# Where the sums of W_down's blocks are made: four sets in attention, eight in mix, two in W_o, none in W_up

## The chip, the cores and the metric

The kernel runs on one core of a Trainium2 chip. The metric is the device time of one execution in microseconds (us), lower is better. Engines are named as in the profile: PE multiplies matrices, DVE is the vector engine, ACT the scalar engine, POOL GpSimd, and SP issues nearly all DMAs of this kernel.

## The reference: one layer of a hybrid decoder

With 512 tokens, a model width of 1024 and a feed-forward width of 4096, all in float32:

```python
h = rms_norm(x, g_pre_mix)
q, k, v, cb, cc, cu, ga, gc = split(h @ w_in)          # 512 x6, 1024 x2
y_attn = stick_breaking_attention(q, k, v) @ w_attn_out  # 8 heads of 64, causal
y_conv = (cb * causal_depthwise_conv(cc * cu, w_conv)) @ w_conv_out
m = sigmoid(ga + b) * y_attn + sigmoid(gc + b) * y_conv
x = x + rms_norm(m @ w_o, g_post_mix)
f = square(relu(rms_norm(x, g_pre_mlp) @ w_up)) @ w_down
x = x + rms_norm(f, g_post_mlp)
x = x + sigmoid(rms_norm(x, g_ple) @ w_ple_gate) * (p @ w_ple_proj)
```

## The kernel before: stages, queues and sums

Every matrix product is split into a high and a low float32r part, three matmuls for one (lines 91 to 93). A weight block of 512 KB is loaded by SP into one of 4 buffers `raw` (line 71); ACT makes the high part `whi` by a cast (line 64), and DVE subtracts to get the low part `wlo` (line 65). The same two lines split everything else: `wth`/`wtl` (the transposed attention weights), `oyh`/`oyl` (the attention output), `st`, `us`. The split weights and the tiles of the sums below share one pool of 15 buffers.

The stages follow each other on PE: the head (norm, v), attention in four steps j of two heads each, mix in eight steps j (gates, convolution and attention output projections), W_o, W_up, W_down, and a last part. W_up and W_down use a Strassen-like scheme with seven products; W_down's right-hand side needs, beside blocks of W_down itself, four sums of blocks for each of 16 sets. `make_sums` (line 296) makes one set, long ahead of W_down: it lets SP issue the saves of the set before (line 292, two of 512 KB from `w` to `wsum` in DRAM), then two loads of 512 KB of `in_w_down_dram` into `w` (line 303), and then the engine that is passed makes four subtractions of 128x512 (line 309).

PE and SP run in program order. On DVE, ACT and POOL a scheduler sets the order when the kernel is built; each of them then runs its list in order, so an instruction that waits for its input holds all that stand behind it. `tc.high_priority(-LATE)` lowers the priority of what is made under it, so that the scheduler puts it behind other work that it thinks ready.

Before the change the 16 sets are made: two in the head and two in attention (steps 1 and 2), all at low priority on DVE; eight in mix, steps 0 and 1 at low priority on DVE, steps 2 to 7 on POOL; three in W_o, one on POOL before block k=0 and one on DVE before k=1 and before k=3; and one on DVE in W_up, in the middle of chunk 4 (the save follows in chunk 6).

What else the prediction speaks of, by its line before the change (from the middle of the attention loop on, lines stand two to ten lower after it). The loop of attention (line 430) makes step j's scores, the convolution, and then the transposes of the two heads' weights (`wtrans`, whose splits are `wth` and `wtl`), with a projection between them to keep PE busy: in the last step, j=3, these are the gates of mix, `gate(0,0)`, `gate(0,1)` and `gate(1,0)` (sigmoid at line 421). `av` (line 388) then multiplies head by head, and line 392 and 393 with a split make `oyh` and `oyl`. In mix, step j takes two gates, one block with the rows of `w_conv_out` and `w_attn_out` (two loads of 256 KB into one `raw`), twelve matmuls of the convolution part, twelve of the attention part and three multiplications and additions (lines 485, 489, 490). Step 0's convolution part is followed by `gate(1,1)`, and then by the attention part, whose last three matmuls use `oyh`, `oyl` of the last two heads. In W_up, `up_load` loads two blocks per chunk and combines them on DVE (669, 671, 672, 673) before they are split into `us`, and after the products DVE adds at lines 695, 701, 703 (and 711 every fourth chunk). Those adds release the PSUM buffers that PE writes next.

Of the kernel before, what the change touches and what calls it, by code (L numbers as in the profile page):

```python
# [25 lines left out]
LATE = 150  # L26
# [7 lines left out]
def hybrid_block(ctx, tc, x, p, g_pre_mix, w_in, b_gate, w_conv, w_attn_out, w_conv_out, w_o,  # L34
                 g_post_mix, g_pre_mlp, w_up, w_down, g_post_mlp, g_ple, w_ple_gate, w_ple_proj, out):
    nc = tc.nc
# [20 lines left out]
    def bank():  # L57
        return psp.tile([P, 512], F32, tag="ps", name="ps")

    def tm(dt=F32):  # L60
        return tmp.tile([P, 512], dt, tag="tmp", name="tmp")
# [18 lines left out]
    def w4(dt=F32):  # L80
        return wts.tile([P, 2, 512], dt, tag="w", name="w4")
# [207 lines left out]
    def save_sums():  # L289
        while unsaved:  # L290
            dst, src = unsaved.pop(0)
            nc.sync.dma_start(dst, src)
# [3 lines left out]
    def make_sums(eng=None):  # L296
        eng = eng or nc.gpsimd
        save_sums()
        j = next(made)
        q = []  # L300
        for h in range(2):
            t = w4()
            nc.sync.dma_start(t, wd[j][h].rearrange("p (c n) -> p c n", c=2))
            q += [t[:, 0], t[:, 1]]
        dst = wsum[j // 2][:, :, j % 2, :]
        o = [w4(), w4()]
        t1, t2, t3, t4 = (o[i // 2][:, i % 2] for i in range(4))
        for r, x_, y_ in ((t1, q[1], q[0]), (t2, q[3], t1), (t3, q[3], q[1]), (t4, q[2], t2)):
            eng.tensor_tensor(r, x_, y_, op=ALU.subtract)
        unsaved.extend([(dst[:, 0:2], o[0]), (dst[:, 2:4], o[1])])  # L310
# [7 lines left out]
    def proj_q(j):  # L318
        st = bigt([P, 4, S], name="st")
        split(st[:, 0], st[:, 1], proj(wcols(w_in, j * P), hx))  # L320
        return st

    def proj_k(j, st):
        split(st[:, 2], st[:, 3], proj(wcols(w_in, 512 + j * P), hx))
# [38 lines left out]
    def wtrans(w):  # L363
        wh = bigt([P, 1280], name="wth")
        wl = bigt([P, 1280], name="wtl")
        for group in ((0,), (1, 3), (2,)):
            ps = bank()
            base = WBLK[group[0]][0]
            n = 0
            for kb in group:  # L370
                c0 = WBLK[kb][0] - base
                for qb in range(kb, NT):
                    o = BLK[qb][0] + kb * P
                    nc.tensor.transpose(ps[:, c0 + (qb - kb) * P:c0 + (qb - kb + 1) * P], w[:, o:o + P], ident)
                n += WBLK[kb][1]
            split(wh[:, base:base + n], wl[:, base:base + n], ps[:, 0:n])
        return wh, wl
# [4 lines left out]
    def av(h, wt, of):  # L382
        ps = bank()
        for kb in range(NT):
            c0, n = WBLK[kb]
            lhs = v2[kb // 2][:, kb % 2, h, :]
            for i in range(2):
                nc.tensor.matmul(ps[:, kb * P:S], lhs, wt[i][:, c0:c0 + n], start=(kb == 0 and i == 0),
                                 stop=(kb == NT - 1 and i == 1))
        r, o = (slice(0, 64), slice(64, 128)) if h % 2 == 0 else (slice(64, 128), slice(0, 64))  # L390
        sh = tm()
        nc.scalar.copy(sh[r], ps[o])
        nc.vector.tensor_tensor(of[r], ps[r], sh[r], op=ALU.add)
        if h % 2 == 1:
            split(oy_h[0][:, h // 2], oy_l[0][:, h // 2], of)

    def conv_c(c):
        ps = proj(wcols(w_in, 2048 + c * P), hx)
        ct = tm()
        nc.scalar.copy(ct, ps)  # L400
        return ct

    def conv_u(c, ct):
        ps = proj(wcols(w_in, 2560 + c * P), hx)
        nc.vector.tensor_tensor(ct, ct, ps, op=ALU.mult)
        y = tm()
        wc = [cols[:, 16 + i * 4 + c:17 + i * 4 + c] for i in range(3)]
        nc.vector.tensor_scalar(y, ct, wc[2], None, op0=ALU.mult)
        for i, d in ((1, 1), (0, 2)):
            nc.vector.scalar_tensor_tensor(y[:, d:S], ct[:, 0:S - d], wc[i], y[:, d:S], op0=ALU.mult, op1=ALU.add)  # L410
        return y

    def conv_b(c, y):
        ps = proj(wcols(w_in, 1536 + c * P), hx)
        nc.vector.tensor_tensor(y, ps, y, op=ALU.mult)
        split(oy_h[1][:, c], oy_l[1][:, c], y)

    def gate(j, which):
        ps = proj(wcols(w_in, 3072 + 1024 * which + j * P), hx)
        sg = tm()  # L420
        nc.scalar.activation(sg, ps, AF.Sigmoid, bias=cols[:, 8 * which + j:8 * which + j + 1])
        return sg
# [9 lines left out]
    for j in range(4):  # L432
        wa, wb = scores(st)
        y = conv_u(j, ct)
        conv_b(j, y)
        if j < 3:
            st = proj_q(j + 1)
        else:
            sg[0] = gate(0, 0)
        ta = wtrans(wa)  # L440
        if j < 3:
            proj_k(j + 1, st)
        else:
            sg[1] = gate(0, 1)
        tb = wtrans(wb)
        if j < 3:
            ct = conv_c(j + 1)
        else:
            next_gate = gate(1, 0)
        of = tm()  # L450
        if j in (1, 2):
            with tc.high_priority(-LATE):
                make_sums(nc.vector)
        av(2 * j, ta, of)
        av(2 * j + 1, tb, of)

# [11 lines left out]
        return lambda k: (oy_h[part][:, k, :], oy_l[part][:, k, :])  # L468

    for j in range(NK):  # L470
        if j > 1:
            make_sums()
        else:
            with tc.high_priority(-LATE):
                make_sums(nc.vector)
        sa, sc = sg if j == 0 else (next_gate if j == 1 else gate(j, 0), last_gate if j == 1 else gate(j, 1))

        def two(t, j=j):
            return [(t[:, 4 * i:4 * i + 4], w[:, j * P:(j + 1) * P].rearrange("(k p) m -> p k m", p=P))
                    for i, w in ((1, w_conv_out), (0, w_attn_out))]  # L480

        wo2 = weights(two, [P, NK, P])
        save_sums()
        py = proj(wo2, oyc(1), 4, 4)
        nc.vector.tensor_tensor(sc, sc, py, op=ALU.mult)
        if j == 0:
            last_gate = gate(1, 1)
        py = proj(wo2, oyc(0), 4, 0)
        nc.vector.tensor_tensor(sa, sa, py, op=ALU.mult)
        nc.vector.tensor_tensor(sa, sa, sc, op=ALU.add)  # L490
        split(m_h[j // 4][:, j % 4], m_l[j // 4][:, j % 4], sa)
        if j == 3:
            for t in range(NT):
                nc.sync.dma_start(xr[t // 2][:, t % 2, :], x[t * P:(t + 1) * P, :])
        if j == 6:
            nc.sync.dma_start(pf, p[0].rearrange("(t p) d -> p t d", p=P))
            nc.sync.dma_start(wpr, w_pp.rearrange("(k p) m -> p k m", p=P))
            split(wph, wpl, wpr)
        if j == 7:
            for kk in range(2):  # L500
                ps = bank()
                for t in range(NT):
                    nc.tensor.transpose(ps[:, t * P:(t + 1) * P], pf[:, t, kk * P:(kk + 1) * P], ident)
                split(pt[:, kk], pt[:, 2 + kk], ps)


    def rows(nk, stat, w, tail, chain):
        acc = {}
        held = {}
        for k in range(nk):  # L510
            if k in (0, 1, 3):
                make_sums(nc.gpsimd if k == 0 else nc.vector)
            if k == 4:
                save_sums()
            wk = wrow(w, k)
            if k >= nk - tail:
                held[k] = wk
                continue
            sh, sl = stat(k)
            for t in range(NT):  # L520
                tok = slice(t * P, (t + 1) * P)
                for hf in range(2):
                    if k == 0:
                        acc[t, hf] = bank()
                    cs = slice(hf * 512, (hf + 1) * 512)
                    mm3(acc[t, hf], sh[:, tok], sl[:, tok], wk[0][:, cs], wk[1][:, cs], k == 0, False)
        for t in range(NT):
            tok = slice(t * P, (t + 1) * P)
            for hf in range(2):
                cs = slice(hf * 512, (hf + 1) * 512)  # L530
                for k in range(nk - tail, nk):
                    sh, sl = stat(k)
                    wk = held[k]
                    mm3(acc[t, hf], sh[:, tok], sl[:, tok], wk[0][:, cs], wk[1][:, cs], False, k == nk - 1)
            chain(t, [acc[t, 0], acc[t, 1]])
# [184 lines left out]
    for _, c, n in order:  # L720
        if n == 6 and c + 1 < NJ:
            up_load(c + 1)
            if c == 4:
                make_sums(nc.vector)
            if c == 6:
                save_sums()
        up_mm(c, n)


# [188 lines left out]
```

## Time and profile before

| what | us |
|---|---|
| median of 3 runs (lowest, highest) | 741.13 (738.96, 741.35) |
| the profiled execution, its own time | 740.71 |
| its span (first to last instruction) | 738.9 |
| PE busy | 727.5 (98%) |
| DVE busy | 515.3 (70%) |
| ACT busy | 378.0 (51%) |
| POOL busy | 98.0 (13%) |

A time in the profile is counted from the start of the span. The timeline gives the start and length of one instruction or of a run of like ones (x3), the engine, the line, what it writes and reads, and in square brackets for how long the engine sat idle before it and what ended that. SPq rows are DMA issues: their length is the time on SP's queue, not that of the transfer. A matmul is pipelined: its length (0.39 us) is longer than the distance to the next one (0.23 us), and the distance is what counts.

### The profile page before, as it was taken

To read this page: it belongs to the slowest core of one execution; us is meant where nothing else is said; L and a number is where in the kernel's file an instruction comes from. 1 tells how busy PE (TensorE), PEld (TensorE's weight loads), DVE (VectorE), ACT (ScalarE), POOL (GpSimd) and SP (SyncE) were. 2 spreads that over 40 slices of the span, in tenths; PEclk is the share of its full clock that TensorE was granted. 3 is DMA by queue.
4 is the path that set the end of the run, shared out by engine and by line. 5 is a ranking of instruction groups with operands and counts; after the bars stand their busy time and mean duration, and the time that the engine had idled before them with its cause. 6 is when DMAs were issued, how large, how long until landed. Compare 5 with 4: busy or idle time off the path is not lost. (4 is left out here: it accounts for less than half of the span.)

```text
span 738.9 us, 10316 instructions
## 1 busy us (share of the span) xinstructions
PE 727.5 (98%) x3976; PEld 630.1 (85%) x3976; DVE 515.3 (70%) x640; ACT 378.0 (51%) x595; POOL 98.0 (13%) x124
## 2 busy tenths in 40 slices
PE   8999999999899999999999999999999999999997
PEld 7888888888688888888899999999988888888886
DVE  6768696967445433844889898967699878268762
ACT  6364546351334221433855696757777467256431
POOL 1105052332442222001100000000000000001100
PEclk9999999999999999999999999999999999999999
DMA  8593717163997867861425544523455767577311
GB/s 313 178 252 112 204 53 228 34 199 120 295 323 254 279 204 256 309 204 65 155 95 169 174 115 115 149 81 93 165 170 177 231 232 225 183 239 273 122 57 58
DMA packets 112105, 132.29 MB, mean 179 GB/s; under 512 B 4116, under 2 KB 82744, under 8 KB 111032
## 3 DMA queue, kind: packets, MB, share of 16 engines
q1 hardware_dynamic: 111464, 127.43, 53.9%
q10 hardware_dynamic: 592, 4.20, 1.4%
q8 instruction: 31, 0.51, 0.3%
q14 instruction: 18, 0.15, 0.1%
HBM read 108.55 MB, written 23.07 MB: 178 GB/s over the span
## 5 line engine op out<-in xcount | busy, mean ns | idle before, releaser
L65 DVE TENSOR_TENSOR wlo<-raw,whi 128x512 fp32r<-128x512 f32 (+1 forms) x84 | 78.4, 955 | 66.5 <-ACT whi L64 41.1
L91 PE MATMUL ps<-h1h,whi 128*128 128x512 f32 x288 | 113.3, 393 | 0.0
L93 PE MATMUL ps<-h1h,wlo 128*128 128x512 f32 x288 | 112.2, 390 | 0.0
L92 PE MATMUL ps<-h1l,whi 128*128 128x512 f32 x288 | 112.2, 389 | 0.0
L64 ACT CAST whi<-raw 128x512 fp32r<-128x512 f32 (+1 forms) x84 | 64.6, 809 | 54.9 <-PE ps L93 20.6
L91 PE MATMUL ps<-w,sb 128*128 128x512 f32 x216 | 84.1, 389 | 0.0
L93 PE MATMUL ps<-w,sb 128*128 128x512 f32 x216 | 84.0, 389 | 0.0
L92 PE MATMUL ps<-w,sb 128*128 128x512 f32 x216 | 84.0, 389 | 0.0
L65 DVE TENSOR_TENSOR w<-raw,w 128x1024 fp32r<-128x1024 f32 x56 | 67.6, 1219 | 21.3 <-PE ps L92 10.2
L64 ACT CAST w<-raw 128x1024 fp32r<-128x1024 f32 x56 | 58.5, 1052 | 34.7 <-PE ps L93 14.1
L133 POOL TENSOR_TENSOR rs<-ms,mhalf 128x1 f32<-128x1 f32 x20 | 14.9, 744 | 419.9 <-DVE ms L129 366.4
L91 PE MATMUL ps<-h2h,us 128*128 128x256 f32 x224 | 63.6, 284 | 1.2 <-DVE tmp L701 1.2
L91 PEld LDWEIGHTS ps<-h1h,whi 128*128 128x128 f32 x288 | 54.1, 188 | 11.5
L93 PEld LDWEIGHTS ps<-h1h,wlo 128*128 128x128 f32 x288 | 54.1, 188 | 11.3
L92 PE MATMUL ps<-h2l,us 128*128 128x256 f32 x224 | 63.4, 283 | 0.0
L93 PE MATMUL ps<-h2h,us 128*128 128x256 f32 x224 | 63.4, 283 | 0.0
L92 PEld LDWEIGHTS ps<-h1l,whi 128*128 128x128 f32 x288 | 54.1, 188 | 10.8
L65 DVE TENSOR_TENSOR us<-raw,us 128x1024 fp32r<-128x1024 f32 x42 | 50.5, 1218 | 6.8 <-ACT us L64 6.7
L64 ACT CAST us<-raw 128x1024 fp32r<-128x1024 f32 x42 | 43.3, 1050 | 19.7 <-DVE raw L673 9.4
L93 PEld LDWEIGHTS ps<-w,sb 128*128 128x128 f32 x216 | 40.5, 188 | 8.5
L92 PEld LDWEIGHTS ps<-w,sb 128*128 128x128 f32 x216 | 40.5, 188 | 8.5
L91 PE MATMUL ps<-tb,us 128*128 128x256 f32 x168 | 47.7, 284 | 0.0
(206 smaller groups left out, 1654.2 us busy)
## 6 DMA issues: line engine op xcount, KB each, us to landing
raw<-in_w_in_dram SPq DMA_DIRECT2D x36, 512.0 KB, 6.4
w<-in_w_down_dram SPq DMA_DIRECT2D x32, 512.0 KB, 4.5
wsum<-w SPq DMA_DIRECT2D x32, 512.0 KB, 3.4
raw<-in_w_up_dram SPq DMA_DIRECT2D x32, 512.0 KB, 4.7
raw<-wsum SPq DMA_DIRECT2D x32, 512.0 KB, 5.2
raw<-in_w_down_dram SPq DMA_DIRECT2D x24, 512.0 KB, 4.1
raw<-in_w_o_dram SPq DMA_DIRECT2D x8, 512.0 KB, 5.8
raw<-in_w_ple_gate_dram SPq DMA_DIRECT2D x8, 512.0 KB, 6.3
```

Of the source, the lines that this page charges most:

```text
L64: a = nc.scalar.copy(hi, src)
L65: b = nc.vector.tensor_tensor(lo, src, hi.bitcast(F32), op=ALU.subtract)
L91: nc.tensor.matmul(ps, lh, rh, start=start, stop=False, skip_group_check=onto)
L92: nc.tensor.matmul(ps, lh, rl, start=False, stop=False, skip_group_check=onto)
L93: nc.tensor.matmul(ps, ll, rh, start=False, stop=stop, skip_group_check=onto)
L133: nc.gpsimd.tensor_tensor(r, m, mhalf, op=ALU.pow)
```

## The change

In attention a set is made in each of the four steps, at normal priority and not at low. In mix the sets stay in the same steps on the same engines, those of steps 0 and 1 at normal priority now. In W_o the set on POOL before block 0 is gone; in W_up the set of chunk 4 and its saves in chunk 6 are gone. There are 16 sets as before; DVE makes 40 subtractions (36 before), POOL 24 (28 before). PE's instructions keep their order.

```diff
@@ attention, end of each step j
         of = tm()
-        if j in (1, 2):
-            with tc.high_priority(-LATE):
-                make_sums(nc.vector)
+        make_sums(nc.vector)
         av(2 * j, ta, of)
         av(2 * j + 1, tb, of)
@@ mix
     for j in range(NK):
-        if j > 1:
-            make_sums()
-        else:
-            with tc.high_priority(-LATE):
-                make_sums(nc.vector)
+        make_sums(nc.gpsimd if j > 1 else nc.vector)
@@ rows(), which W_o uses
-            if k in (0, 1, 3):
-                make_sums(nc.gpsimd if k == 0 else nc.vector)
+            if k in (1, 3):
+                make_sums(nc.vector)
@@ W_up
         if n == 6 and c + 1 < NJ:
             up_load(c + 1)
-            if c == 4:
-                make_sums(nc.vector)
-            if c == 6:
-                save_sums()
         up_mm(c, n)
```

Three places show what the scheduler makes of it. The first is SP's list at the end of attention. Before the change it holds there, from the gate block of `gate(1,1)` on, the sets of mix 1 (`w_1920`, `w_1922`, saved as `w_1924`, `w_1925`) and mix 2 (`w_1972`, `w_1974`), and, at the line with x2, the blocks of `gate(2,0)` and `gate(2,1)`:

```order
L71 DMA raw<-in_w_in_dram 128x8x128
L303 DMA w_1920<-in_w_down_dram 128x1024
L303 DMA w_1922<-in_w_down_dram 128x1024
L71 DMA raw<-in_w_conv_out_dram 128x4x128
L71 DMA raw<-in_w_attn_out_dram 128x4x128
L292 DMA wsum_377<-w_1924 128x2x512
L292 DMA wsum_377<-w_1925 128x2x512
L303 DMA w_1972<-in_w_down_dram 128x1024
L303 DMA w_1974<-in_w_down_dram 128x1024
L71 DMA raw<-in_w_in_dram 128x8x128 x2
L71 DMA raw<-in_w_conv_out_dram 128x4x128
L71 DMA raw<-in_w_attn_out_dram 128x4x128
```

After the change, from the gate block of `gate(1,1)` on, which here too stands behind the saves of mix 0's set, with mix 1's set (`w_1944`, `w_1946`, saved as `w_1948`, `w_1949`) and mix 2's (`w_1996`, `w_1998`):

```order
L71 DMA raw<-in_w_in_dram 128x8x128
L303 DMA w_1944<-in_w_down_dram 128x1024
L303 DMA w_1946<-in_w_down_dram 128x1024
L71 DMA raw<-in_w_conv_out_dram 128x4x128
L71 DMA raw<-in_w_attn_out_dram 128x4x128
L292 DMA wsum_378<-w_1948 128x2x512
L292 DMA wsum_378<-w_1949 128x2x512
L303 DMA w_1996<-in_w_down_dram 128x1024
L303 DMA w_1998<-in_w_down_dram 128x1024
L71 DMA raw<-in_w_in_dram 128x8x128 x2
L71 DMA raw<-in_w_conv_out_dram 128x4x128
L71 DMA raw<-in_w_attn_out_dram 128x4x128
```

The rows read alike, since the list is the same from here on; but one set more (that of attention's step 3) stands ahead of it now, so that mix 0's set stands in time where mix 1's stood, and the block of `gate(1,1)` and all that follows come one set later. The blocks of `gate(2,0)` and `gate(2,1)` still follow the saves of mix 1's set and the loads of mix 2's.

The second place is ACT's list at the end of attention, from the sigmoid of `gate(0,0)` (the first row at line 421) on. There are two groups of `wth` (heads 6 and 7), and `whi` of 128x1024 are gate blocks. Before:

```order
L421 ACTIVATE tmp<-ps,cols 128x512
L64 CAST wth<-ps 128x512 x2
L64 CAST wth<-ps 128x256
L64 CAST whi<-raw 128x1024
L421 ACTIVATE tmp<-ps,cols 128x512
L64 CAST wth<-ps 128x512 x2
L64 CAST wth<-ps 128x256
L64 CAST whi<-raw 128x1024
```

After, from the row ahead of that sigmoid on:

```order
L64 CAST whi<-raw 128x1024
L421 ACTIVATE tmp<-ps,cols 128x512
L64 CAST wth<-ps 128x512 x2
L64 CAST wth<-ps 128x256
L64 CAST whi<-raw 128x512 x2
L421 ACTIVATE tmp<-ps,cols 128x512
L64 CAST wth<-ps 128x512 x2
L64 CAST wth<-ps 128x256
L421 ACTIVATE tmp<-ps,cols 128x512
L64 CAST whi<-raw 128x1024
L392 COPY tmp<-ps 64x512
L64 CAST whi<-raw 128x1024
```

The first `whi` of 128x1024 is now the block of `gate(1,1)`, ahead of the sigmoid. Between the two groups of `wth` stood the block of `gate(2,0)`; now the block of mix 1's `w_conv_out` and `w_attn_out` stands there, and the two blocks of `gate(2,0)` and `gate(2,1)` follow behind, on both sides of a copy of the last heads' output.

The third place is DVE's list in W_up around the set that is removed (`w_3764`, `w_3766`). Before:

```order
L65 TENSOR_TENSOR us<-raw,us 128x1024
L309 TENSOR_TENSOR w_3768<-w_3764 128x512
L711 TENSOR_TENSOR af<-af 128x4x256
L309 TENSOR_TENSOR w_3768<-w_3766,w_3768 128x512
L309 TENSOR_TENSOR w_3769<-w_3766,w_3764 128x512
L309 TENSOR_TENSOR w_3769<-w_3766,w_3768 128x512
L701 TENSOR_TENSOR tmp<-ps,tmp 128x256
L65 TENSOR_TENSOR us<-raw,us 128x1024
L695 TENSOR_TENSOR tmp<-ps,tmp 128x256
L669 TENSOR_TENSOR s_3879<-raw 128x512
```

After, two chunks further on (lines 663, 665 to 667, 689, 695 are before's 669, 671 to 673, 695, 701; the first column of sums of a chunk is `s`):

```order
L65 TENSOR_TENSOR us<-raw,us 128x1024 x2
L665 TENSOR_TENSOR raw<-s_4004,raw 128x512
L65 TENSOR_TENSOR us_4016<-s_4004,us_4016 128x512
L666 TENSOR_TENSOR raw<-raw 128x512
L667 TENSOR_TENSOR raw<-raw 128x512
L663 TENSOR_TENSOR s_4127<-raw 128x512
L65 TENSOR_TENSOR us<-raw,us 128x1024
L695 TENSOR_TENSOR tmp<-ps,tmp 128x256
L65 TENSOR_TENSOR us<-raw,us 128x1024
L689 TENSOR_TENSOR tmp<-ps,tmp 128x256
```

The four subtractions are gone, and the scheduler puts the first step of the next chunk's loads (`s`, which waits for a DMA) ahead of the adds at 695 and 689 of the chunk that PE is working on.

## The prediction

> **What bounds the kernel now.** I read the page's head first, then PE's waits, then the work in windows of 20 us, then the timeline where a window is short of work. The page says that PE is the bound:
>
> ```profile
> span 738.9 us, 10316 instructions
> PE 727.5 (98%) x3976; PEld 630.1 (85%) x3976; DVE 515.3 (70%) x640; ACT 378.0 (51%) x595; POOL 98.0 (13%) x124
> ```
>
> So a subtraction that is moved between DVE, POOL and stages costs or saves nothing in itself. Only PE's waits count. The list of PE's waits, longest first, names those that the change can reach:
>
> ```profile
> PE ps L388 <- ACT wth L64: 1.9, 1, 1.9
> ...
> PE ps L91 <- DVE tmp L701: 1.2, 2, 0.6
> PE ps L388 <- DVE wtl L65: 1.1, 1, 1.1
> ```
>
> Two places: the product of head 7 at the end of attention (line 388), called stall A here, and the add at line 701 in W_up, stall B. The windows (PE busy and matmuls, PEld, DVE, ACT, POOL, granted clock, DMA share, GB/s) show that A costs more than its idle time:
>
> ```profile
> 180.00:200.00 20.00, 16.99 (x77) 14.02 (x76) 10.19 (x15) 7.46 (x13) 6.84 (x6) 0.91 0.91 286
> ...
> 181.00:193.00 12.00, 8.99 (x45) 7.29 (x44) 4.17 (x7) 4.60 (x8) 5.03 (x4) 0.97 1.08 333
> ```
>
> 3.0 us are idle in the first window, at a mean clock of 0.91. PE's timeline through A:
>
> ```profile
> 187.26 0.39 PE L388 MATMUL ps<-wth,v 128*128 128x512 f32 x1
> ...
> 188.36 0.27 PE L388 MATMUL ps<-wtl,v 128*128 128x128 f32 x1
> 190.56 0.50 PE L388 MATMUL ps<-wth,v 128*128 128x512 f32 x1 [1.93 <-ACT wth L64]
> 192.15 0.69 PE L388 MATMUL ps<-wtl,v 128*128 128x512 f32 x1 [1.08 <-DVE wtl L65]
> ...
> 194.02 0.73 PE L91 MATMUL ps<-oyh,whi 128*128 128x512 f32 x1
> 194.55 0.63 PE L92 MATMUL ps<-oyl,whi 128*128 128x512 f32 x1
> ...
> 196.01 0.40 PE L93 MATMUL ps<-oyh,wlo 128*128 128x512 f32 x1
> 196.25 0.40 PE L91 MATMUL ps<-oyh,whi 128*128 128x512 f32 x1
> ```
>
> Head 6's eight matmuls run from 187.26 to the next start at about 188.43, 1.17 us. Head 7's would do the same and end at 189.60; five matmuls at the normal distance (0.23, 196.01 to 196.25) would bring the sixth of mix to 190.75. It starts at 196.01. Stall A costs 5.3 us: 3.0 idle, 2.3 of matmuls spaced 0.3 to 0.5 us until 195.8.
>
> Its cause is an order. ACT, DVE and SP at that place:
>
> ```profile
> 178.33 0.68 ACT L421 ACTIVATE tmp<-ps,cols 128x512 f32<-128x512 f32 x1
> 178.91 1.33 ACT L64 CAST wth<-ps 128x512 fp32r<-128x512 f32 x3
> 188.40 1.04 ACT L64 CAST whi<-raw 128x1024 fp32r<-128x1024 f32 x1 [8.15 <-DMA raw<-in_w_in_dram]
> ...
> 189.94 1.33 ACT L64 CAST wth<-ps 128x512 fp32r<-128x512 f32 x3
> ```
>
> ```profile
> 179.49 0.68 DVE L309 TENSOR_TENSOR w<-w,w 128x512 f32<-128x512 f32 x1
> 180.09 1.61 DVE L65 TENSOR_TENSOR wtl<-ps,wth 128x512 fp32r<-128x512 f32 x3
> 189.54 1.95 DVE L65 TENSOR_TENSOR wlo<-raw,whi 128x1024 fp32r<-128x1024 f32 x1 [7.83 <-ACT whi L64]
> 191.41 1.60 DVE L65 TENSOR_TENSOR wtl<-ps,wth 128x512 fp32r<-128x512 f32 x3
> ```
>
> ```profile
> 175.94 4.63 SPq L292 DMA_DIRECT2D wsum<-w  x2
> 180.62 1.34 SPq L303 DMA_DIRECT2D w<-in_w_down_dram  x2
> 182.05 1.07 SPq L71 DMA_DIRECT2D raw<-in_w_in_dram  x2
> ```
>
> ACT sits 8.15 us before the cast of the block of gate(2,0), with head 7's `wth` behind it in the list. That block was issued at 182.05 and landed at 188.40. SP stood ahead of it at the second save of mix 1's set until the last subtraction of that set had ended (179.49 + 0.68 = 180.17; the save went out by 180.57). So a set's last sum, late on DVE, holds SP, SP holds a gate's block, the block holds ACT, and ACT holds head 7.
>
> **The change part by part.** *Stall A.* The rows of the new order put head 7's `wth` behind the block of w_conv_out and w_attn_out of mix 1, not behind that of gate(2,0), and one set earlier on SP. My walk through the new lists, on before's clock: the two scans with their products,
>
> ```profile
> 162.34 2.88 DVE L354 TENSOR_TENSOR_SCAN keep<-keep,ends 128x1280 f32<-128x1280 f32 x1 [0.68 <-POOL keep L351]
> ...
> 171.31 1.49 DVE L355 TENSOR_TENSOR beta<-beta,keep 128x1279 f32<-128x1279 f32 x1 [0.61 <-POOL beta L351]
> ```
>
> take 10.5 us. A `wlo` of 1.2 us is no longer ahead of them, so they run from about 161.0 to 171.5; two short steps of the convolution and mix 0's last sum follow and end at 172.6 to 173.3. The save goes out, gate(1,1)'s block leaves at 173.7 and mix 1's loads behind it. What such transfers take:
>
> ```profile
> DMA to landing us min/median/max: 4.2/5.2/8.4
> ...
> DMA to landing us min/median/max: 2.7/3.7/5.3
> ```
>
> (the first row is that of the weight blocks between 150 and 200 us, the second that of the sums' loads and saves there). With 1.0 MB of saves, 0.5 of gate block, 1.0 of loads and 0.5 of the mix block at 333 GB/s, behind each other, gate(1,1) lands at 178.5, mix 1's two loads at 180.2 and 181.8, its block by 183.4. ACT then casts that block and does head 7's `wth` (1.33) by about 186.0; they are due at 188.4, where head 7 follows head 6. DVE makes the four sums of mix 1 between 182.5 and 184.9, two `wlo` of 0.6, and the first piece of `wtl` by 187.4, due at 188.66. The slack is 2.4 us on ACT and 1.3 on DVE. Stall A goes: **-5.3 us**.
>
> What would come of gate(1,1)'s block standing ahead of gate(0,0)'s sigmoid: that sigmoid frees a bank for gate(1,0). It ran at 178.33 before and would now end at 180.0. gate(1,0), 24 matmuls of 0.23 us ahead of head 6 at 187.26, starts at 181.7: no cost, with 1.7 us of slack.
>
> A rule against this size: the Trainium skill (TensorE: Matmul & The Clock Gate, What's actually happening) has the clock fall to half only after an idle window of about 3.4 us. By that rule two waits of 1.93 and 1.08 us with matmuls between would leave the clock alone, A would cost 3.0 and the forecast would be 2.3 us higher, 737.8. The rows disagree: 0.53 us from 194.02 to 194.55, with no wait there. The sum goes by the rows.
>
> *A new wait in mix 0.* The last three matmuls of its attention part read `oyh`, `oyl` of heads 6 and 7. On before's clock:
>
> ```profile
> 205.34 0.39 PE L92 MATMUL ps<-oyl,whi 128*128 128x512 f32 x1
> ```
>
> That is the matmul that reads that `oyl`; without A it stands at 205.34 - 5.3 = 200.0. Before, the split was done early:
>
> ```profile
> 198.03 0.69 DVE L65 TENSOR_TENSOR oyl<-tmp,oyh 128x512 fp32r<-128x512 f32 x1 [0.69 <-ACT oyh L64]
> ```
>
> Now that `oyh` stands on ACT behind both blocks of gate(2,.) and behind mix 2's, which SP sends after mix 1's saves and mix 2's loads: 7 transfers of 0.524 MB from 184.9 on, 3.67 MB. At 333 GB/s they are through by 195.9, and a last one lands some 1.8 us after its bytes' share (the median of 3.7 less 1.6 for 0.524 MB at 333 GB/s is 2.1, the shortest, 2.7, gives 1.1): 197.7. Then the cast, `oyh` and `oyl`, at some 0.7 us each with the hand-over: 199.9, and the matmul waits for a little of `oyl` or nothing. At the 286 GB/s of the first window it is 201.7 and the wait 1.7. I take **+0.5**, in a range of 0 to 2. By the Trainium skill (DMA: Bandwidth & Descriptors, Where 436 GB/s comes from) transfers between HBM and SBUF are bound at about 358 GB/s for a core; by that, an estimate from the page, the bytes would take 10.3 us and not 11.0, the term would be 0 and the forecast 735.0. The best stretch here shows 333 GB/s, so the sum keeps its 0.5.
>
> *W_up.* The rows of stall B:
>
> ```profile
> 484.70 0.28 PE L93 MATMUL ps<-tb,us 128*128 128x256 f32 x1
> 485.63 0.39 PE L91 MATMUL ps<-h2h,us 128*128 128x256 f32 x1 [0.65 <-DVE tmp L701]
> ...
> 495.68 0.28 PE L93 MATMUL ps<-tb,us 128*128 128x256 f32 x1
> 496.54 0.39 PE L91 MATMUL ps<-h2h,us 128*128 128x256 f32 x1 [0.59 <-DVE tmp L701]
> ```
>
> ```profile
> 476.27 1.22 DVE L65 TENSOR_TENSOR us<-raw,us 128x1024 fp32r<-128x1024 f32 x1
> ...
> 483.22 0.69 DVE L669 TENSOR_TENSOR s<-raw 128x512 f32<-128x512 f32 x1 [2.56 <-DMA raw<-in_w_up_dram]
> ...
> 485.15 0.42 DVE L701 TENSOR_TENSOR tmp<-ps,tmp 128x256 f32<-128x256 f32 x1
> ```
>
> The distance is 0.12 us, so B costs 0.93 - 0.12 = 0.81 and 0.86 - 0.12 = 0.74, together 1.55. DVE frees a raw buffer at 477.49, the load lands at 483.2, and the add that PE needs stands behind the `s` that waits for it. DVE runs behind PE here, so four sums of 0.60 to 0.69 fewer (2.6 us, with the two loads and two saves of that set) bring the chain 2 to 4 us earlier, if nothing on the way waits for PE. I give that 60%. Against it stands the new order: `s` of the next chunk now comes ahead of the adds at 695 and 701 from chunk 6 on, and in my walk one of those adds is 0.4 to 1.0 us late at about 435 us. Bounds: -1.55 to +1.0. I take **-0.8**.
>
> *At nothing.* Step 0 of attention, whose set is new there, has room for its four sums on DVE:
>
> ```profile
> 57.17 2.88 DVE L354 TENSOR_TENSOR_SCAN keep<-keep,ends 128x1280 f32<-128x1280 f32 x1 [3.32 <-POOL keep L351]
> ```
>
> They take 2.6 of those 3.32 us, ahead of the scan. On SP the set's saves and loads come ahead of five weight blocks, the first of which PE needs five projections later (24 matmuls of 0.23 us each, 27 us in all). If that cover fails, the scan is late by what the loads are late, and the projections between scan and transposes hide that first. W_o: PE has no wait there in the list above, and the set on POOL that goes held nothing that PE waited for; its removal gives nothing and costs nothing.
>
> The sum against the profiled execution: 740.71 - 5.3 + 0.5 - 0.8 = 735.1. The median of the runs is 0.42 above that execution, so 735.5.
>
> **The rivals.**
>
> *The wait moves to mix 0 and eats most of the gain* (0.14). For it: seven transfers stand ahead of that `oyh` where five do before the `whi` that A waits for. If the stretch runs at 260 GB/s or mix 1's sums end 2 us later, PE idles 3 us there, and with 1 us of slow clock that is +4: 740.71 - 5.3 + 4 - 0.8 = 738.6, 739.0 against the median. Against it: 333 GB/s over the 12 us in which the same kinds of transfer run now.
>
> *Stall A stays, behind another cast* (0.10). Head 7's `wth` still stands behind a load. If mix 1's block lands at 186 and not 183.4, ACT's slack of 2.4 is used up, and 3 us more give A back: 740 to 742. Against it: of the weight blocks there the slowest took 8.4 us, and this one has 12.3 from gate(1,1)'s issue on.
>
> *W_up takes the other end* (0.18). B stays and the new add waits 1.0: 740.71 - 5.3 + 0.5 + 1.0 = 736.9, 737.3 against the median.
>
> *Slower* (0.08): DVE's four sums of mix 1 now stand ahead of head 7's `wtl`, and wait for mix 1's loads. They decide everything behind: the save, mix 2's loads, both gate blocks, `oyh`. If the loads land 6 us late (after 187.8, not 181.8), head 7 waits about 4.7 us for `wtl` and mix 0 some 2 us more, with 2.3 of slow clock: +9.0 against -5.3 - 0.8: 743.6, 744.0 against the median. It needs mix 0's last sum at 179, behind both scans, where it now has 172.6 to 173.3. The whole chain of two scans takes 10.5 us now; it would have to take 16.
>
> That the change does nothing is part of the second rival: the total of sums is the same, and every other stage has no wait to lose.
>
> **How the numbers follow.** The forecast case has 0.50, the rivals 0.14, 0.10, 0.18 and 0.08. 0.3%, 2.2 us here, is about what a measurement of this kernel can tell from no change; that is 738.9 against the median. Faster: the forecast, W_up's other end, half of the moved wait: 0.75. Same: the other half and two thirds of A staying: 0.14. Slower: the rest, 0.11. The low end takes all of B (-0.75), no new wait (-0.5) and a set of runs that falls as low as the lowest of the three shown (2.2 below the median, of which I take 1.8): 732.5. The high end reaches past the moved wait to the stay of A, 740.8.
>
> **What would show it.** Right: no wait at line 388 near 188 us; mix's first matmul near 189.6; granted clock 1.00 in 180 to 200. The cast of gate(1,1) at about 178.5, and a wait, if any, at line 92 near 200 us with `oyl` as its releaser. In W_up the waits at line 701 (695 now) at 485 and 496 are gone or stand elsewhere. Wrong: a wait at line 388 as before, a wait of over 2 us near 200, or a wait of PE in attention's first three steps.

## The result, and the profile after

Five runs of each: 736.22 us median after the change (735.63 to 736.28), 741.13 before (738.96 to 741.71). The ratio is 0.9936, with a 95% interval of 0.992 to 0.9951: faster by 0.5 to 0.8%. The forecast was 735.5, in a range of 732.5 to 740.8. The profiled execution took 735.77 us, its span is 4.9 us shorter. (Of the experiments further down, one execution of e10, 1210.47 us, and one of the kernel before, 1867.48 us, ran far slower than all others and are left out of the ratios.) The head of the changed kernel's page:

```profile
span 734.0 us, 10311 instructions
...
PE 725.5 (99%) x3976; PEld 628.9 (86%) x3976; DVE 518.3 (71%) x644; ACT 379.3 (52%) x595; POOL 93.8 (13%) x120
```

PE's waits after the change (line, what was waited for, total, times, longest):

```profile
PE ps L91 <- DVE st L65: 0.9, 1, 0.9
...
PE ps L92 <- DVE oyl L65: 0.7, 1, 0.7
```

The waits at lines 388 and 701 are gone. Two that were not there before have come. Since PE runs the same matmuls in the same order, each one's start can be set against its start before; where the difference jumps, time was won or lost. This ledger has the first matmul behind each jump, from the two timelines:

| place | before | after | after less before | step |
|---|---|---|---|---|
| head | 9.77 | 9.93 | +0.16 | +0.16 |
| attention step 0, wait for `st` | 78.85 | 80.13 | +1.28 | +1.12 |
| end of attention, stall A gone | 196.71 | 192.94 | -3.77 | -5.05 |
| mix 0, wait for `oyl` | 205.34 | 202.45 | -2.89 | +0.88 |
| after W_o | 359.75 | 357.01 | -2.74 | +0.15 |
| W_up, line 701 | 485.63 | 482.07 | -3.56 | -0.82 |
| W_up, line 701 | 496.54 | 492.15 | -4.39 | -0.83 |
| last part, wait for `wlo` | 703.20 | 698.31 | -4.89 | -0.50 |

Two things help to read it. The idle time that the profile gives counts from the end of the matmul before (0.39 us behind its start), while the next could have started 0.23 us behind it, so a wait steps the ledger by 0.16 us more than its idle time. And the matmul behind a wait can be late too: 0.10 of the step of the row "after W_o" is there already at 205.57, so the wait in mix 0 costs about 1.0; in the same way 0.1 of the last row belongs to W_up, which makes W_up -1.75 and the last part -0.4.

The windows of the two stretches around the end of attention (columns as before), to be read beside those of before with 16.99 us of PE and a clock of 0.91:

```profile
180.00:200.00 20.00, 20.00 (x100) 16.93 (x99) 12.06 (x17) 10.47 (x18) 5.08 (x4) 1.00 0.88 284
200.00:220.00 20.00, 19.27 (x85) 15.65 (x84) 11.72 (x16) 6.86 (x11) 5.30 (x5) 1.00 1.03 340
```

**Stall A.** SP, ACT and PE of the changed kernel, which is 1.3 us late on before's clock at that place:

```profile
173.70 0.37 SPq L292 DMA_DIRECT2D wsum<-w  x1
174.16 0.41 SPq L71 DMA_DIRECT2D raw<-in_w_in_dram  x1
174.67 1.52 SPq L303 DMA_DIRECT2D w<-in_w_down_dram  x2
```

```profile
179.54 1.05 ACT L64 CAST whi<-raw 128x1024 fp32r<-128x1024 f32 x1 [2.09 <-DMA raw<-in_w_in_dram]
...
183.02 1.27 ACT L64 CAST whi<-raw 128x512 fp32r<-128x512 f32 x2 [0.61 <-DMA raw<-in_w_conv_out_dram]
184.20 0.68 ACT L421 ACTIVATE tmp<-ps,cols 128x512 f32<-128x512 f32 x1
184.78 1.34 ACT L64 CAST wth<-ps 128x512 fp32r<-128x512 f32 x3
```

```profile
189.66 0.27 PE L388 MATMUL ps<-wtl,v 128*128 128x128 f32 x1
189.78 0.44 PE L388 MATMUL ps<-wth,v 128*128 128x512 f32 x1
```

gate(1,1)'s block is cast at 179.54, mix 1's at 183.02, and head 7's `wth` ends at 186.1. PE goes from head 6 to head 7 without a gap.

**Mix 0.** ACT, DVE and PE:

```profile
194.81 1.05 ACT L64 CAST whi<-raw 128x1024 fp32r<-128x1024 f32 x1 [5.30 <-DMA raw<-in_w_in_dram]
...
199.59 0.62 ACT L64 CAST whi<-raw 128x512 fp32r<-128x512 f32 x1
200.50 0.62 ACT L64 CAST oyh<-tmp 128x512 fp32r<-128x512 f32 x1 [0.29 <-DVE tmp L393]
```

```profile
201.71 0.68 DVE L65 TENSOR_TENSOR oyl<-tmp,oyh 128x512 fp32r<-128x512 f32 x1
```

```profile
202.45 0.50 PE L92 MATMUL ps<-oyl,whi 128*128 128x512 f32 x1 [0.73 <-DVE oyl L65]
```

The last heads' `oyh` stands behind four casts of weight blocks, the first of which waits 5.30 us for its load.

**Attention step 0.** SP's list, ACT, DVE, and PE's wait:

```profile
42.49 1.62 SPq L292 DMA_DIRECT2D wsum<-w  x2
48.42 0.82 SPq L303 DMA_DIRECT2D w<-in_w_down_dram  x2
49.34 9.01 SPq L71 DMA_DIRECT2D raw<-in_w_in_dram  x5
```

```profile
55.65 1.05 ACT L64 CAST whi<-raw 128x1024 fp32r<-128x1024 f32 x1 [2.10 <-DMA raw<-in_w_in_dram]
56.60 0.59 ACT L347 ACTIVATE keep<-ps 128x512 f32<-128x512 f32 x1
```

(the same sigmoid before the change:)

```profile
54.23 0.60 ACT L347 ACTIVATE keep<-ps 128x512 f32<-128x512 f32 x1
```

```profile
53.26 1.89 DVE L309 TENSOR_TENSOR w<-w,w 128x512 f32<-128x512 f32 x3 [0.64 <-DMA w<-in_w_down_dram]
56.73 1.22 DVE L65 TENSOR_TENSOR wlo<-raw,whi 128x1024 fp32r<-128x1024 f32 x1 [1.58 <-ACT whi L64]
60.49 2.88 DVE L354 TENSOR_TENSOR_SCAN keep<-keep,ends 128x1280 f32<-128x1280 f32 x1 [2.53 <-POOL keep L351]
```

```profile
80.13 0.50 PE L91 MATMUL ps<-h1h,whi 128*128 128x512 f32 x1 [0.88 <-DVE st L65]
```

The set's loads wait on SP until 48.42, so the next weight block can be cast only at 55.65. ACT has that cast ahead of the first sigmoid of the step (56.60, before 54.23) and the cast of one more block between the sigmoids (57.57), and the scan starts at 60.49 where it started at 57.17. DVE's list behind it is 2 to 5 us later, the `st` that PE needs at 79 by 4.1 us (79.39, before 75.28).

### The profile page after: what moved, and what is told of

It is laid out like the page before. It is cut to its first block, busy times and chain, and to the rows that moved or that the text cites. A ratio compares the mean times of both kernels' runs of the same rounds, so it can differ in the third digit from the quotient of the medians.

```text
span 734.0 us, 10311 instructions
## 1 busy us (share of the span) xinstructions
PE 725.5 (99%) x3976; PEld 628.9 (86%) x3976; DVE 518.3 (71%) x644; ACT 379.3 (52%) x595; POOL 93.8 (13%) x120
## 4 chain that ended last, share of the span: by engine, by line
PE 96%; DVE 1%; DMA 1%; ACT 1%; issue 0%; POOL 0%; DVEq 0%; SPq 0%; ACTq 0%; POOLq 0%
PE ps L91 30%; PE ps L92 30%; PE ps L93 30%; DMA raw<-in_w_conv_out_dram 1%; PE ps L340 1%; PE ps L388 1%; PE ps L374 1%; PE ps L182 1%; DVE wlo L65 1%; PE ps L568 1%; PE ps L141 0%; PE ps L201 0%; PE ps L223 0%; ACT whi L64 0%; PE ps L497 0%
```

## The experiments

Each was run beside the kernel before on the same chip, and its ratio is to that. The ledger of each profile, PE's starts against those of before, is used as above.

**The priority alone (e1).** The kernel before, with the low priorities taken off in attention and mix:

```diff
         if j in (1, 2):
-            with tc.high_priority(-LATE):
-                make_sums(nc.vector)
+            make_sums(nc.vector)
...
-        if j > 1:
-            make_sums()
-        else:
-            with tc.high_priority(-LATE):
-                make_sums(nc.vector)
+        make_sums(nc.gpsimd if j > 1 else nc.vector)
```

> The kernel before with the low priority taken off in attention and in mix steps 0 and 1; all sets stay where they were. My theory: the stall at the end of attention goes because one set more stands ahead in SP's list, not because of the priority. Here only one sum of mix 1's set moves ahead of two other steps on DVE, so SP is let go about 1.8 us sooner, and the blocks of gate(2,0) and now also gate(2,1) still stand ahead of head 7's weights on ACT: the stall stays, 3 to 5 us of its 5.1, and both waits at line 701 in W_up stay. Time 739 to 741 (ratio 0.997 to 1.000). Rival: the priority removes the stall: 736.0 (ratio 0.993).

739.48 against 739.9, ratio 0.999 (0.9978 to 1.0003). ACT at the end of attention:

```profile
186.69 1.05 ACT L64 CAST whi<-raw 128x1024 fp32r<-128x1024 f32 x1 [6.20 <-DMA raw<-in_w_in_dram]
188.92 1.04 ACT L64 CAST whi<-raw 128x1024 fp32r<-128x1024 f32 x1 [1.18 <-POOL w L309]
189.87 0.68 ACT L421 ACTIVATE tmp<-ps,cols 128x512 f32<-128x512 f32 x1
190.45 1.34 ACT L64 CAST wth<-ps 128x512 fp32r<-128x512 f32 x3
```

The first gate block comes 1.7 us sooner (188.40 before), as SP is let go 1.6 us sooner, but a second one now stands ahead of head 7's `wth`, which is no earlier. (The second row names POOL; the chain that ended last has that block's load there, issued at 180.96 and landed at 188.46.) By the ledger 0.6 of the 5.05 us go. The priority does not remove stall A.

**The extra set alone (e2).** The kernel before, all low priorities kept, `if j in (1, 2, 3)` in attention and no set in W_up.

> The kernel before with the set of W_up moved to step 3 of attention, all low priorities kept, W_o as before. My theory: the extra set alone removes the stall of 5.1 us, the two waits in W_up (1.65) and a small one at 703 us (0.5); the last sum of mix 0's set is some 2.6 us later than in the changed kernel, so gate(0,0)'s sigmoid is late and gate(1,0) may wait 0 to 1 us near 182; oyh stands ahead of gate(2,1)'s block on ACT, so no wait in mix 0; no wait at 80 us. Sum 734.0 to 735.0, ratio 0.990 to 0.992. Rival, the priority does it: the stall stays, 738.5 to 739.

735.7 against 739.9, ratio 0.9939 (0.9924 to 0.9955), a little above the expected 0.990 to 0.992. Stall A is gone, there is no wait in mix 0, and the wait for the sigmoid of gate(0,0) has come, 0.88 in the ledger:

```profile
182.91 0.50 PE L91 MATMUL ps<-h1h,whi 128*128 128x512 f32 x1 [0.62 <-ACT tmp L421]
```

So it is the set more in attention, one place in SP's list, that takes A away; the normal priority trades this wait for that in mix 0: e3, which comes next, is e2 with the normal priorities. It acts through mix 0's set, whose last sum ends at 175.2 in e2 and at 173.7 in the changed kernel, and lets SP send the block of gate(1,1) that much later or sooner.

**Step 0's set put back to W_o (e3).**

```diff
-        make_sums(nc.vector)
+        if j > 0:
+            make_sums(nc.vector)
         av(2 * j, ta, of)
...
-            if k in (1, 3):
-                make_sums(nc.vector)
+            if k in (0, 1, 3):
+                make_sums(nc.gpsimd if k == 0 else nc.vector)
```

> The changed kernel with the set of attention's step 0 put back to W_o (POOL, ahead of block 0). My theory: the wait for st at 80 us (1.12 of offset) goes and nothing else changes: the wait for oyl in mix 0 (0.88) stays, W_o has no wait. 735.1, ratio 0.992. Rival: that set has to be made somewhere and W_o pays: a wait of PE near 300 us of 1 us or more, 736 or above.

735.69, ratio 0.994 (0.9926 to 0.9954), where 0.992 was expected. The wait at 80 us is gone and W_o has none, but mix 0 now waits twice:

```profile
200.89 0.49 PE L91 MATMUL ps<-oyh,whi 128*128 128x512 f32 x1 [0.51 <-ACT oyh L64]
202.16 0.50 PE L92 MATMUL ps<-oyl,whi 128*128 128x512 f32 x1 [0.78 <-DVE oyl L65]
```

In the ledger these are 1.69 where the changed kernel has 0.88. The matmul that needs `oyl` starts at nearly the same time as in the changed kernel (202.16 against 202.45): what PE wins at 80 us it waits for at 200. My expectation that nothing else would change was wrong.

**Who makes step 0's sums (e4).** The changed kernel with `make_sums(nc.vector if j else nc.gpsimd)` in attention.

> The changed kernel with the four sums of attention's step 0 on POOL and not on DVE; its loads and saves stay where they are on SP. My theory of the wait for st at 80 us: the set's saves and loads hold the next weight block back on SP, ACT has that block's cast ahead of the first sigmoid of step 0, and so the scan is late; who makes the sums does not matter. The wait stays, 0.8 to 1.2 us of offset, scan of step 0 at 60 us or later. Rival: DVE's four sums ahead of the scan make it late: the wait goes, scan at about 57 to 58.

737.19, ratio 0.9957 (0.9942 to 0.9972). The wait stays, 1.27 us idle; the scan is as late with no sum ahead of it on DVE:

```profile
57.41 1.23 DVE L65 TENSOR_TENSOR wlo<-raw,whi 128x1024 fp32r<-128x1024 f32 x1 [7.19 <-ACT whi L64]
61.10 2.89 DVE L354 TENSOR_TENSOR_SCAN keep<-keep,ends 128x1280 f32<-128x1280 f32 x1 [2.47 <-POOL keep L351]
```

So the set's transfers and the order on ACT make it late, not DVE's 2.6 us. Transfers and order were not tried apart here.

**Step 0's set put back to W_up (e5).** As e3, but W_o as in the changed kernel, and the set at c == 4 and its save at c == 6 of W_up as before.

> The changed kernel with the set of attention's step 0 put back to W_up (chunk 4, saved in chunk 6); W_o without its POOL set. The sum beside e3 is the price of a set in W_up against one on POOL in W_o. My prediction's theory: the two waits in W_up come back, 0.8 to 1.6 us slower than e3: 736.5 to 737.3. Rival: those waits are the landing time of a weight block, which scatters from run to run by as much: within 0.5 us of e3, 735.2 to 736.2.

736.22, ratio 0.9937 (0.9919 to 0.9955), beside 0.994 of e3: no difference, but the intervals (1.3 us to each side) are too wide to part the two theories by the time alone. The profile does it: it lists no wait of PE in W_up at all, with the set there (waits under 0.15 us are not listed; there is one of 0.14). The waits at that add, in the profiles of all kernels: with the set in W_up 1.24 us (before), 0.2 (e1), 0.8 (e7), 0 (e5), 0.4 (e13); without it 0 (the changed kernel), 0.6 (e2), 0.3 (e3), 0.2 (e4), 0.3 (e8), and 0 three times (e9, e11, e12). Means of 0.5 and 0.2, with a scatter as large; e1, e5, e7 and e13 have before's lists on DVE and ACT in W_up, to the instruction. By the ledgers e1, e5 and e13 win 1.1 to 1.3 us in W_up with the set in place, where the changed kernel wins 1.75 without it; e7 wins 0.4. The first wait follows the landing of one block, since the steps on DVE behind it run without a gap: issued at 477.52 before, it took 5.68 us to land, and issued at 477.04 in e1, 4.83.

**Mix 2's blocks held (e8, e9).** e8 is e3, e9 the changed kernel, each with

```diff
         for i in range(parts):
             sl = slice(i * n, (i + 1) * n)
-            split(hi[:, sl], lo[:, sl], raw[:, sl])
+            with tc.issue_after(held_by[0]) if held_by else nullcontext():
+                split(hi[:, sl], lo[:, sl], raw[:, sl])
...
-        av(2 * j + 1, tb, of)
+        last_oy = av(2 * j + 1, tb, of)
...
+        if j == 2:
+            held_by.append(last_oy[0].ins)
```

in `weights`, attention and mix; the hold ends behind mix 2's blocks, and `av` returns its split.

> The kernel of e3 with the casts and subtractions of mix 2's blocks (gate(2,0), gate(2,1), w_conv_out and w_attn_out) held until the output of the last two heads has been split; all DMAs, PE and POOL in the same order. My theory: the wait for oyl in mix 0 is this order on ACT and nothing else: the 0.9 us go, 734.2, ratio 0.991, and no new wait at mix 2. Rival: oyl is late because PE and DVE make it late: time as e3, 735.1.

> The changed kernel with the casts and subtractions of mix 2's blocks held until the output of the last two heads has been split; the set of attention's step 0 stays. My theory: only the wait for oyl in mix 0 goes (0.88 of offset), the wait for st at 80 us stays (1.12): 735.2 to 735.6, some 0.9 us under the changed kernel and 0.5 to 1.1 over e8. Rival: the wait moves on to mix 1, where the held blocks are late: time as the changed kernel.

e8: 734.26, ratio 0.9926 (0.9911 to 0.9941); e9: 735.38, ratio 0.9934 (0.9915 to 0.9954). In both profiles the wait in mix 0 is gone and none has come in mix 1 or 2; e9 keeps the wait for `st` (1.12 us idle). The intervals of e8 and e3 overlap, but e8's median is 1.43 us below that of e3, in the same runs.

**The stall by itself (e7, e10, e13).** e7 is the kernel before with mix 1's sums on POOL and, by the same edit, at normal priority (`if j > 0: make_sums()`).

> The kernel before with one change: the sums of mix 1's set on POOL, which is free from 171 us on, and not on DVE. No set is moved. My theory of the stall at the end of attention: SP stands at the save of mix 1's set until its last sum, late on DVE, is done. POOL has it done at about 176.5, not 180.2, so the gate blocks land some 3.5 us sooner and head 7's weights are in time by about 1 us: the stall of 5.1 goes (0 to 1 us stays), W_up as before: 735.0 to 737 where before has 740 to 741 (ratio 0.993 to 0.995). Rival: the stall is the order on ACT or the DMA rate alone; the gate blocks, two of them now ahead of head 7's weights, hold them as long: ratio 0.998 to 1.000.

739.23 against 740.65, ratio 0.9985 (0.9971 to 0.9998). The stall stays, 2.4 us idle; the expected time did not come. POOL was done at 178.4, not 176.5, since it and DVE slowed each other (last section), so SP was let go only 1.7 us sooner; and as in e1 two gate blocks stood ahead of head 7's `wth`, the second cast at 188.89. e7 does not part the theories. e10 does: the kernel before with the hold of e8 and e9 and no set moved.

> The kernel before with all sets and priorities as they were; only the casts and subtractions of mix 2's blocks (gate(2,0), gate(2,1), w_conv_out and w_attn_out) are held until the output of heads 6 and 7 has been split. All DMAs, PE and POOL keep their order. My theory: the stall at the end of attention is the gate block's cast ahead of head 7's weights on ACT and of its subtraction on DVE, nothing else; it goes whole, 5.1 us: 735 to 736 where before has 740 to 741, ratio 0.992 to 0.994, as much as the whole change. Rival: the DMA or DVE's sums would hold head 7 anyway: ratio above 0.997.

> The kernel of e10 once more, for a profile at full clock. By the theory no wait at line 388 and none near 200 us; head 7's wth cast right behind the sigmoid of gate(0,1), by 184; gate(2,0)'s cast behind the last heads' oyh, after 193; the blocks' landing as before, at 188. PE's offset against the kernel before about -5.2 from 196 us on; in W_up the waits at line 701 may be there or not, as the set is. 734 to 735, ratio 0.990 to 0.993. Rival: part of the stall stays at line 388 for want of wtl: an offset of less than 4.

734.26 against 740.76, ratio 0.9913 (0.9898 to 0.9928); and again, as e13, 734.77 against 740.64, ratio 0.9923 (0.9905 to 0.9941). SP and ACT of e13 (line 64 as before, 73 is before's 71):

```profile
182.26 1.07 SPq L73 DMA_DIRECT2D raw<-in_w_in_dram  x2
```

```profile
181.89 1.34 ACT L64 CAST wth<-ps 128x512 fp32r<-128x512 f32 x3
...
191.74 0.62 ACT L64 CAST oyh<-tmp 128x512 fp32r<-128x512 f32 x1 [0.76 <-DVE tmp L396]
192.27 3.03 ACT L64 CAST whi<-raw 128x1024 fp32r<-128x1024 f32 x4
```

gate(2,0)'s block is issued at 182.26, as late as before (182.05), and head 7's `wth` is done at 183.2. From there on PE's starts are 5.1 us further ahead than at the transposes. Stall A is the order of two casts on ACT (the hold moves their subtractions on DVE as well), with the late load only behind it.

**W_up's set moved to W_o (e11, e12).** The kernel before, and e10, with

```diff
-            if k in (0, 1, 3):
-                make_sums(nc.gpsimd if k == 0 else nc.vector)
+            if k < 4:
+                make_sums(nc.vector if k % 2 else nc.gpsimd)
...
-            if c == 4:
-                make_sums(nc.vector)
-            if c == 6:
-                save_sums()
```

> The kernel before with the set of W_up made in W_o, on POOL ahead of block 2; attention and mix untouched. My prediction had two waits of W_up, 1.55 to 1.65 us, go with that set: 739.0 or so where before has 740.5, ratio 0.998. Rival, after the runs so far: the waits at line 701 depend on when one weight block lands, and come and go in executions of the same list; without the set they are smaller by 0.3 us or so on the mean: ratio 0.999 to 1.000. The stall at the end of attention stays in both.

> Both together: the kernel before with mix 2's blocks held, and W_up's set made in W_o on POOL ahead of block 2. No stall at the end of attention, no wait at 80 us, none in mix 0. By the theory 734 to 735, ratio 0.991 to 0.993, level with e8 (734.3) and 1 to 2 us under the changed kernel. Rival: a wait in W_o for POOL's second set, 736 or more.

743.29 against 740.76, ratio 1.0038 (1.0024 to 1.0052), and 738.46, ratio 0.9963 (0.9949 to 0.9977): slower than with the set in W_up, which no theory of e11 expected (e12's rival did, from another wait). Both have no wait in W_up, and both have new ones behind W_o: 0.56 us for `hf`, and then, for the normalised rows (line 557):

```profile
363.24 1.29 PE L574 MATMUL ps<-ident,tmp 128*128 128x128 f32 x8 [2.09 <-DVE tmp L557]
```

In e11 DVE starts that chain at 341.70, where it started at 338.23 before; ahead of it in its list now stands W_up's first `s`, which waits for a load until 338.94, and behind that a `us`. By e11's ledger 3.7 us are lost there between 348 and 363, and 1.7 won in W_up. Whether that order or the later loads of W_o is the cause was not tried by itself.

## Why the prediction was right

**Stall A (-5.3, measured -5.05).** Right in mechanism and size, the 2.3 us of matmuls spaced wider included: with no wait before them they run at 0.23 us and a granted clock of 1.00. The walk had gate(1,1)'s block at 178.5 and head 7's `wth` done by 186.0 on before's clock; they came at 178.2 and 184.8. e2 shows that the extra set does it, e10 that the order on ACT is the stall.

**The new wait in mix 0 (+0.5, measured +0.88, about 1.0 with the matmul behind it).** Right in place and kind. The last block landed at 199.04, 197.7 on before's clock, as the walk had it, but `oyl` ended at 202.4, 201.1 on before's clock, not 199.9. The walk left out what else stands there: a copy of the heads' output (line 392) ahead of the last cast, the addition (line 393) that `oyh` waits for, and on DVE a `wlo` ahead of `oyl`.

**"At nothing" in step 0 (0, measured +1.12).** This step failed. It counted DVE's room for four sums and the 27 us until the blocks are needed, and said that the projections would hide a late scan. The blocks' casts stand ahead of sigmoids on ACT, so a block that nobody needs for 27 us held the scan by 3.3 us, and the delay reached PE as a late `st`. I had looked for what waits for the load, not for what waits behind the cast; the same fault as stall A's, in another stage. e4 rules out DVE's sums as the cause. A wait in attention's first three steps was one of the prediction's own signs of being wrong, and it came.

**W_up (-0.8, measured -1.65 in the profile).** The measured step is a little past the lower bound, but not for the reason given. The argument that the set's 2.6 us on DVE make these waits did not hold: e5 has the set and no wait, e1 the same list and a sixth of it. The first of them hangs on when one weight block lands, and that moved by 0.85 us between two kernels with the same lists there. By the means above I estimate that the part of the gain that lasts is nearer to 0.3 than to 1.65; that -0.8 lies between the two is luck. The wait that the new order was to bring near 435 us did not come.

**The sum.** -5.3 + 0.5 - 0.8 = -5.6 was forecast, -4.9 came. On the one side stand the 1.1 us missed at step 0, some 0.5 more at mix 0, 0.25 less at A and 0.16 in the head; on the other 0.95 more in W_up and 0.4 in the last part, for which the prediction has no term. That last wait is 0.2 us idle before, 0.5 in e7, 0.3 in e11, 0.8 in e13 and none in the other profiles, though no edit reaches that part. So the sum came out this close by luck in its small terms; its large term, stall A, is no luck. Of the rivals, the moved wait came in small, as its own term; the slower one did not: mix 1's sums ended at 185.9 and `wtl` was in time.

**What the experiments add.** The end of attention could have been had without moving a set: e10 is level with e8, and 1 to 2 us below the changed kernel by their medians (734.3 to 734.8 against 736.2, not in the same runs, so by the ratios: 0.9913 and 0.9923 against 0.9936, with intervals that overlap). In e13's ledger 5.1 us of the gain are stall A and 1.1 W_up's waits, and 0.8 are lost again in the last part.

## What to carry to other kernels

An engine that runs a list in order holds all that stands behind a wait, so for each load that is moved, look at what stands behind its first reader, not at when the data is needed. If a stall is two instructions in the wrong order, order those two by a dependency; moving other work until the scheduler happens to turn them round costs new waits elsewhere. And before a small wait is put down to a cause, look at it in profiles of several executions: most of what this change seemed to win in W_up came in profiles that keep the set there (e1, e5, e13).

## What the runs showed of the hardware

**POOL's sums beside DVE.** In e7 POOL makes three subtractions while DVE works on two-input steps of the convolution:

```profile
171.60 2.57 DVE L355 TENSOR_TENSOR beta<-beta,keep 128x1279 f32<-128x1279 f32 x1 [0.61 <-POOL beta L351]
...
175.63 3.36 DVE L410 SCALAR_TENSOR_TENSOR tmp<-tmp,cols 128x511 f32<-128x511 f32 x2
```

```profile
172.90 5.54 POOL L309 TENSOR_TENSOR w<-w,w 128x512 f32<-128x512 f32 x3
...
184.80 3.78 POOL L309 TENSOR_TENSOR w<-w,w 128x512 f32<-128x512 f32 x3
```

The product took 1.49 before, the two steps at 410 some 1.5 together; POOL's three take 3.78 with DVE idle (up to their last 0.8 us) and 5.54 here. The Trainium skill (GPSIMD Engine Reference, Specifications) says that GpSimd shares its SBUF interface with VectorE, with contention where a VectorE instruction has two SBUF inputs; these rows agree, and both sides pay.

**The clock after a wait.** The same wait of 2.09 us for line 557 (563 in e12) was followed by matmuls 0.23 us apart in e11 and 0.43 apart in e12. PE of e12, then of e11:

```profile
358.25 1.29 PE L580 MATMUL ps<-ident,tmp 128*128 128x128 f32 x8 [2.09 <-DVE tmp L563]
359.29 0.64 PE L94 MATMUL ps<-wph,pt 128*128 128x512 f32 x1
359.73 0.63 PE L95 MATMUL ps<-wpl,pt 128*128 128x512 f32 x1
...
362.29 0.63 PE L95 MATMUL ps<-wpl,pt 128*128 128x512 f32 x1
362.72 0.46 PE L96 MATMUL ps<-wph,pt 128*128 128x512 f32 x1
```

```profile
364.59 0.39 PE L92 MATMUL ps<-wpl,pt 128*128 128x512 f32 x1
364.82 0.39 PE L93 MATMUL ps<-wph,pt 128*128 128x512 f32 x1
```

The windows there, from 2.2 us before the wait's end to 5.8 behind it (granted clock behind the engines' times), of e12 and of e11:

```profile
356.00:364.00 8.00, 5.88 (x23) 4.57 (x23) 6.80 (x13) 6.63 (x15) 1.86 (x2) 0.79 0.30 98
```

```profile
361.00:369.00 8.00, 5.88 (x30) 4.75 (x30) 7.04 (x15) 7.26 (x17) 1.87 (x3) 1.00 0.31 98
```

The clock fell to 0.79 in the one and stayed at 1.00 in the other. So in these two profiles the same wait cost 1.5 us more or nothing more, while waits of 0.5 to 0.9 us cost at most 0.2 beyond their idle time and the 0.16 of the ledger's note. The scatter of a kernel's runs does not follow such waits: it is 3.8 us in e12 and 1.5 in e11, which have one, and 4.8 in e4 and 3.9 in e9, which have none.
